# One core, two decoder layers: the weights' split into high and low parts, in two pieces a chunk instead of four

## The chip, the core and the metric

The kernel runs on one core of a Trainium2 chip. The metric is device time in microseconds (us) of one execution of the program; the figure given for a kernel is the median of its runs. The engines are called as the profile calls them: PE (TensorE, matmuls), PEld (its weight loads), DVE (VectorE), ACT (ScalarE), POOL (GpSimd) and SP (SyncE, which here only issues DMAs).

## The reference

A decoder trunk of two layers on x of shape (1, 256, 2048) in float32. Cut to what matters:

```python
for layer in range(2):
    if layer % 2 == 0:      # RG-LRU heads and RWKV-7 heads side by side
        h = rms_norm(x, even_norm)
        xa, ga, pb = split(h @ w_in)             # w_in: 2048 x 5408
        ya = rg_lru(causal_dwconv(xa), ...) * gelu(ga)
        yb = rwkv7_time_mix(pb, ...)             # 16 heads of 64
        x = x + concatenate([ya, yb]) @ w_out    # 2048 x 2048
    else:                   # mLSTM, chunkwise
        h = rms_norm(x, odd_norm)
        xm, z = split(h @ w_in)                  # 2048 x 8192
        q, k, v = block_diag(...)                # blocks of 4
        hs = head_layer_norm(mlstm_chunkwise(q, k, v, ...)) + skip * silu(causal_dwconv(xm))
        x = x + (hs * silu(z)) @ w_out           # 4096 x 2048
    h = rms_norm(x, ffn_norm)                    # gated FFN with a causal convolution
    u = silu(causal_dwconv(h @ w_gate)) * (h @ w_up)   # 2048 x 5632, twice
    x = x + u @ w_down                           # 5632 x 2048
out = rms_norm(x, final_norm)
```

Nearly all of the arithmetic is in the big projections, and each weight is used once.

## The kernel before

Activations lie transposed, features on the 128 partitions and the 256 positions along the free axis. Weights come from HBM in *chunks* of 128 x 2048 float32 (1 MB), 416 of them: 40 for the even layer's input projection (`ein`), 8 + 8 for its output projection (`eoa`, `eob`), 2 x 88 for gate and up (`fgu`), 2 x 44 for down (`fd`), 64 and 32 for the odd layer's input and output (`oin`, `oout`). A chunk holds 16 tiles of 128 columns; a tile is the stationary operand of the matmuls of one pair of a row block k and a column block m.

The matmuls take operands in a reduced float32 format (F32R). To keep the precision, a weight w is split into a high part `wh` (w cast to F32R, on ACT) and a low part `wl` (w - wh, on DVE), and an activation likewise. Three products are added: high x high, high x low and low x high. `mm3` does this for a tile; the activation's two parts stand side by side, so that one matmul of 512 columns with `wh` (L254, L257) gives two products and one of 256 columns with `wl` (L255) the third. In the narrow form, used when only 256 positions of PSUM are there for a sum, `wh` is used twice with 256 columns (L259, L260) and `wl` once (L261). `mm3_pair` (L311, L313) does two tiles at a time for the FFN.

`chunk` loads one chunk by a DMA on SP's queue into a `raw` buffer (two of them), and `parts_of` gives the `wh` and `wl` buffers (a pool of two each) and a function that splits the piece i of the chunk. `chunk` splits all pieces one after the other. A buffer of `wh` or `wl` comes free when PE has read its last tile. `load_x`, at the start, calls `parts_of` itself, with four pieces of 288 columns.

Callers of `chunk` are `project` (16 tiles, k = 0 to 15, into one output), `flat` (the output projections; for `eoa` and `eob` an output takes 8 tiles, so a chunk holds two outputs) and `flat_pairs` (FFN). After every four tiles, or every two pairs, they call `tick`, which advances the other work by a step: generators for the RWKV pairs, the RG-LRU, the convolutions and the mLSTM heads. So the program is written in an order in which the small work is interleaved with the tiles; the lists `WAITS`, `OWAITS` and so on at the head of the file say how many ticks each step lets pass.

The framework's scheduler then decides by a cost estimate of its own in which order each engine gets its instructions, and sets the semaphores. So the order on DVE, ACT and PE may differ from the order in the code, and depends on the instructions' sizes.

Small operations of the even layer that the prediction names: L593 to L617 prepare an RWKV pair (two heads) from its projections, and L596 is a PE matmul of that preparation, whose result L598 reads; L629 and L630 copy `uv` out of PSUM, for PE's L637 and L649; L651 to L658 build the blocks for the triangular inverse; L765 to L772 normalise a pair's output `y` (the variance `var`, its root `rsq` on POOL, L381); L409 is a tap of a convolution (`lru_x`), which PE's L822 (the RG-LRU gates) needs; L824 to L843 are the RG-LRU's own rows; L432 adds an output tile to the residual `res`; L201 and L202 split an activation into its two parts.

Of the kernel before, what the change touches and what calls it, by code (L numbers as in the profile page):

```python
# [42 lines left out]
WAITS = [2, 6, 1, 0, 2, 6, 12, 1, 1, 0, 1, 1, 1, 7]  # L43
ZSTEP = 7
EWIDE = False
PIECES = 4
SW = [4, 2]
OWAITS = [5, 2, 4]
AWAITS = [0, 4, 0, 1, 1, 3]
# [57 lines left out]
class Builder:  # L107
# [118 lines left out]

    def chunk(self, src, n=2048, pieces=PIECES):
        hi, lo, piece = self.parts_of(self.raw_load(src, n), pieces)
        for i in range(pieces):
            piece(i)  # L230
        return hi, lo
# [992 lines left out]
```

## Time and profile before

| | us |
|---|---|
| runs, not profiled | 2627.35, 2628.34, 2629.81 (median 2628.34) |
| the profiled execution's own time | 2631.14 |
| its span, first to last instruction | 2629.4 |

The stages follow one another in time, since each needs the whole of the one before:

| stage | us of the span |
|---|---|
| even layer, input projection with RWKV and RG-LRU | 0 to 380 |
| even layer, output projection | 380 to 517 |
| first FFN, up and down | 517 to 985, 985 to 1222 |
| odd layer, input projection with mLSTM, output projection | 1222 to 1700, 1700 to 1885 |
| second FFN, up and down | 1885 to 2372, 2372 to 2614 |
| final norm and output | 2614 to 2629.4 |

How to read the rows quoted below. A row of the timeline is: start and duration in us, engine, line of the kernel, operation, what it writes and reads, shapes, count, and in brackets how long the engine had been idle before it and which operation released it. A group's row ends with the number of instructions, their busy time in us, the mean of one in ns, and the idle time before them by what ended it. A row of waits is: total us, times, longest. In the rows by window the first two numbers are the stretch and its length, then each engine's busy time with its instructions, then the granted TensorE clock (1.00 is full speed), the DMA engines' busy share and GB/s.

### The profile page before, as it was taken

How to read it: one execution, taken by the hardware profiler on the slowest of the kernel's cores; microseconds unless marked ns; L12 is line 12 of the kernel's file. 1: busy time of each engine (PE TensorE's matmuls, PEld its weight loads, DVE VectorE, ACT ScalarE, POOL GpSimd, SP SyncE). 2: the span in 40 equal slices, each digit the busy share in tenths (PEclk: the TensorE clock that was granted, in tenths of full speed). 3: DMA queues.
4: the chain of work that ended last, by engine and by line, in shares of the span. 5: the costliest groups of instructions: out<-in, count | busy, mean ns of one | idle time of the engine just before them, and what ended most of it. 6: DMA issues, size and time to landing. Idle time of an engine off the chain costs nothing.

```text
span 2629.4 us, 42787 instructions
## 1 busy us (share of the span) xinstructions
PE 2600.2 (99%) x16214; PEld 2274.5 (87%) x16214; DVE 1865.2 (71%) x4261; ACT 1466.4 (56%) x3094; POOL 140.5 (5%) x417
## 2 busy tenths in 40 slices
PE   9999999999999999999999999999999999999997
PEld 8988887888888888888888888888888888888886
DVE  7988888888677765555777688865666667775554
ACT  6766663555555554444666667644455555554443
POOL 1222220000000000000000000000000000000000
PEclk9999999999999999999999999999999999999998
DMA  5433333455555555555444444455555555555553
GB/s 207 154 123 125 118 102 137 173 214 212 187 185 190 188 184 202 190 189 189 161 145 145 143 147 161 145 192 187 182 192 192 192 183 188 191 187 198 181 201 131
DMA packets 67694, 454.37 MB, mean 173 GB/s; under 512 B 9328, under 2 KB 10352, under 8 KB 14240
## 3 DMA queue, kind: packets, MB, share of 16 engines
q1 hardware_dynamic: 62064, 441.69, 47.6%
q0 software_dynamic: 4416, 7.85, 1.2%
q8 instruction: 127, 2.08, 0.3%
q10 hardware_dynamic: 1008, 2.11, 0.2%
q14 instruction: 79, 0.65, 0.1%
HBM read 448.70 MB, written 2.10 MB: 171 GB/s over the span
## 4 chain that ended last, share of the span: by engine, by line
PE 71%; issue 10%; DVE 0%; ACT 0%; POOL 0%; DVEq 0%; POOLq 0%; ACTq 0%
PE mp L311 31%; PE mp L313 15%; PE mm L257 14%; PE mm L255 8%; PE sc L934 1%; PE mm L254 1%; PE pv L919 1%; PE pz L1074 1%; PE pr L928 1%; PE pz L1075 0%; DVE res L1119 0%; PE pz L1052 0%; PE pt L397 0%; PE pt L1088 0%; PE pt L1065 0%
## 5 line engine op out<-in xcount | busy, mean ns | idle before, releaser
L244 DVE TENSOR_TENSOR wl<-raw,wh 128x512 fp32r<-128x512 f32 (+1 forms) x1680 | 1094.3, 684 | 506.2 <-ACT wh L243 505.3
L243 ACT CAST wh<-raw 128x512 fp32r<-128x512 f32 (+1 forms) x1680 | 956.0, 618 | 711.4 <-PE mp L311 510.9
L311 PE MATMUL mp<-x,wh 128*128 128x512 f32 x2816 | 884.7, 395 | 0.0
L313 PEld LDWEIGHTS mp<-x,wl 128*128 128x128 f32 x2816 | 529.0, 188 | 125.0
L313 PE MATMUL mp<-x,wl 128*128 128x256 f32 x2816 | 553.2, 278 | 0.0
L311 PE MATMUL mp<-ux,wh 128*128 128x512 f32 x1408 | 437.0, 392 | 0.0
L311 PEld LDWEIGHTS mp<-x,wh 128*128 128x128 f32 x2816 | 428.8, 189 | 0.1
L257 PE MATMUL mm<-x,wh 128*128 128x512 f32 x960 | 341.7, 394 | 0.0
L313 PEld LDWEIGHTS mp<-ux,wl 128*128 128x128 f32 x1408 | 264.4, 188 | 58.2
L255 PE MATMUL mm<-x,wl 128*128 128x256 f32 x1024 | 283.4, 287 | 0.0
L313 PE MATMUL mp<-ux,wl 128*128 128x256 f32 x1408 | 277.9, 279 | 0.0
L257 PE MATMUL mm<-yx,wh 128*128 128x512 f32 x720 | 259.5, 399 | 0.0
L255 PE MATMUL mm<-yx,wl 128*128 128x256 f32 x768 | 212.3, 287 | 1.9 <-DVE wl L244 1.0
L311 PEld LDWEIGHTS mp<-ux,wh 128*128 128x128 f32 x1408 | 213.2, 188 | 0.0
L257 PEld LDWEIGHTS mm<-x,wh 128*128 128x128 f32 x960 | 180.3, 188 | 35.9 <-DVE x L344 0.2
L255 PEld LDWEIGHTS mm<-x,wl 128*128 128x128 f32 x1024 | 193.2, 189 | 7.6 <-DVE yx L202 2.3
L259 PE MATMUL mm<-x,wh 128*128 128x256 f32 x640 | 193.2, 302 | 0.0
L261 PE MATMUL mm<-x,wl 128*128 128x256 f32 x640 | 182.5, 285 | 1.5 <-DVE wl L244 1.5
L260 PE MATMUL mm<-x,wh 128*128 128x256 f32 x640 | 181.4, 283 | 0.0
L257 PEld LDWEIGHTS mm<-yx,wh 128*128 128x128 f32 x720 | 137.1, 191 | 29.4
L255 PEld LDWEIGHTS mm<-yx,wl 128*128 128x128 f32 x768 | 145.9, 191 | 7.9 <-DVE wl L244 1.4
L259 PEld LDWEIGHTS mm<-x,wh 128*128 128x128 f32 x640 | 121.7, 190 | 6.7 <-ACT wh L243 0.2
(352 smaller groups left out, 2640.2 us busy)
## 6 DMA issues: line engine op xcount, KB each, us to landing
raw<-fgu SPq DMA_DIRECT2D x176, 1024.0 KB, 4.9
raw<-fd SPq DMA_DIRECT2D x88, 1024.0 KB, 4.8
raw<-oin SPq DMA_DIRECT2D x64, 1024.0 KB, 4.8
raw<-ein SPq DMA_DIRECT2D x40, 1024.0 KB, 5.0
raw<-oout SPq DMA_DIRECT2D x32, 1024.0 KB, 4.8
raw<-eoa SPq DMA_DIRECT2D x8, 1024.0 KB, 4.8
raw<-eob SPq DMA_DIRECT2D x8, 1024.0 KB, 4.8
wif<-wif POOLq DMA_DIRECT2D x12, 256.0 KB, 4.3
```

The costliest lines, as they stand in the source:

```text
L243: nc.scalar.copy(hi[:, s], raw[:, s])
L244: nc.vector.tensor_tensor(out=lo[:, s], in0=raw[:, s], in1=hi[:, s].bitcast(F32), op=ALU.subtract)
L254: TE.matmul(ps, hi, x, start=True, stop=False)
L255: TE.matmul(ps[:, 1], lo, x[:, 1], start=False, stop=False)
L257: TE.matmul(ps, hi, x, start=False, stop=stop)
L259: TE.matmul(ps, hi, x[:, 0], start=start, stop=False)
L260: TE.matmul(ps, hi, x[:, 1], start=False, stop=False)
L261: TE.matmul(ps, lo, x[:, 1], start=False, stop=stop)
L311: TE.matmul(ps[:, i], hi[i], x, start=start, stop=False)
L313: TE.matmul(ps[:, i, 1], lo[i], x[:, 1], start=False, stop=stop)
L919: TE.matmul(ps[:, s], xm[:, 3 + s * P:3 + s * P + P], bv, start=True, stop=True)
L928: TE.matmul(ps, bl, xc, start=True, stop=True)
```

## The change

`PIECES` is the default of `chunk`'s argument `pieces`: a chunk of 2048 columns is split in two pieces of 1024 columns, where it was four of 512. `load_x` is not touched.

```diff
 EWIDE = False
-PIECES = 4
+PIECES = 2
 SW = [4, 2]
 ...
     def chunk(self, src, n=2048, pieces=PIECES):
         hi, lo, piece = self.parts_of(self.raw_load(src, n), pieces)
         for i in range(pieces):
             piece(i)
         return hi, lo
```

On ACT and on DVE there are 832 instructions fewer each. The DMAs and PE's 15229 rows are the same in number, but the scheduler orders what lies between differently: some 570 of PE's rows stand at another place, by at most 32 places, nearly all of them in the even layer, and 995 of DVE's other rows, by at most 17. Three places on DVE follow, first as before, then as changed. The last two numbers of a name are buffer numbers and differ between the two.

At the first RWKV pair, some 60 us into the span, DVE before. `wl_112` is the chunk on which PE works; its first piece stands further up in both.

```order
L610 TENSOR_TENSOR ar_104_855<-r_81_722,ep_96_810 128x4x64
L604 SCALAR_TENSOR_TENSOR t0_103_852<-a_94_803,k_79_716 128x256
L605 SCALAR_TENSOR_TENSOR k_79_716<-t0_103_852,vec_sb_70,k_79_716 128x256
L598 TENSOR_SCALAR t1_102_847<-pw_101_845 128x256
L613 TENSOR_TENSOR bk_105_856<-k_79_716,epi_97_813 128x4x64
L617 SCALAR_TENSOR_TENSOR t1_106_863<-r_81_722,vec_sb_70,k_79_716 128x256
L244 TENSOR_TENSOR wl_112_886<-raw_110_883,wh_111_885 128x512 x3
L409 SCALAR_TENSOR_TENSOR lru_x_114_908<-xa_84_764,vec_sb_70,lru_x_114_908 128x256
L601 TENSOR_TENSOR kk_99_817<-kk_99_817,t1_102_847 128x256
```

The same place, DVE as changed:

```order
L610 TENSOR_TENSOR ar_104_835<-r_81_706,ep_96_790 128x4x64
L604 SCALAR_TENSOR_TENSOR t0_103_832<-a_94_783,k_79_700 128x256
L244 TENSOR_TENSOR wl_112_866<-raw_110_863,wh_111_865 128x1024
L598 TENSOR_SCALAR t1_102_827<-pw_101_825 128x256
L605 SCALAR_TENSOR_TENSOR k_79_700<-t0_103_832,vec_sb_70,k_79_700 128x256
L409 SCALAR_TENSOR_TENSOR lru_x_114_884<-xa_84_748,vec_sb_70,lru_x_114_884 128x256
L613 TENSOR_TENSOR bk_105_836<-k_79_700,epi_97_793 128x4x64
L617 SCALAR_TENSOR_TENSOR t1_106_843<-r_81_706,vec_sb_70,k_79_700 128x256
L409 SCALAR_TENSOR_TENSOR lru_x_114_884<-xa_84_748,vec_sb_70,lru_x_114_884 128x256
L244 TENSOR_TENSOR wl_127_960<-raw_125_957,wh_126_959 128x1024
```

The second piece of the chunk has moved up from behind L617 to right behind L604, and it now holds the tiles k = 8 to 15, where before the second held k = 4 to 7. On PE, L596 stood behind the tile k = 3 and now stands behind k = 8; the L822 that follow stand five tiles later than before.

At the end of the RWKV pair at 240 us, DVE before (`wl_545` is the current chunk, `y_475` the pair's output):

```order
L244 TENSOR_TENSOR wl_545_3395<-raw_543_3392,wh_544_3394 128x512
L765 TENSOR_TENSOR y_475_3007<-y_475_3007,st_536_3362 128x256
L427 TENSOR_TENSOR ga_540_3386<-mm_531_3310,bc_69_653 128x256
L244 TENSOR_TENSOR wl_545_3395<-raw_543_3392,wh_544_3394 128x512
L769 TENSOR_REDUCE var_538_3368<-lnsq_537_3366 128x4
L409 SCALAR_TENSOR_TENSOR lru_x_551_3429<-xa_527_3295,vec_sb_70,lru_x_551_3429 128x256
L770 TENSOR_SCALAR var_538_3368<-var_538_3368 128x4
L696 TENSOR_TENSOR zf_572_3537<-zc_493_3145,con_even_sb_358 128x512
L772 TENSOR_TENSOR y_475_3007<-y_475_3007,rsq_539_3371 128x256
L629 COPY uv_549_3421<-pw_550_3422 64x2x64
L409 SCALAR_TENSOR_TENSOR lru_x_551_3429<-xa_527_3295,vec_sb_70,lru_x_551_3429 128x256
L629 COPY uv_549_3421<-pw_550_3422 64x2x64
```

The same place, DVE as changed:

```order
L244 TENSOR_TENSOR wl_545_3295<-raw_543_3292,wh_544_3294 128x1024
L612 TENSOR_TENSOR bk_523_3173<-kk_512_3115,epi_510_3111 128x4x64
L765 TENSOR_TENSOR y_475_2919<-y_475_2919,st_536_3262 128x256
L427 TENSOR_TENSOR ga_540_3286<-mm_531_3210,bc_69_637 128x256
L409 SCALAR_TENSOR_TENSOR lru_x_551_3325<-xa_527_3199,vec_sb_70,lru_x_551_3325 128x256
L769 TENSOR_REDUCE var_538_3268<-lnsq_537_3266 128x4
L409 SCALAR_TENSOR_TENSOR lru_x_551_3325<-xa_527_3199,vec_sb_70,lru_x_551_3325 128x256
L770 TENSOR_SCALAR var_538_3268<-var_538_3268 128x4
L629 COPY uv_549_3317<-pw_550_3318 64x2x64
L772 TENSOR_TENSOR y_475_2919<-y_475_2919,rsq_539_3271 128x256
L409 SCALAR_TENSOR_TENSOR lru_x_551_3325<-xa_527_3199,vec_sb_70,lru_x_551_3325 128x256
L629 COPY uv_549_3317<-pw_550_3318 64x2x64
```

The two narrow pieces around L765 have become one wide piece ahead of it, L612 has come in, the 512-column L696 has gone elsewhere, and one of the two copies of `uv` stands ahead of L772.

At the start of the output projection, 387 us, DVE before (`wl_933` is the first chunk of `eoa`; its first piece stands further up in both):

```order
L653 TENSOR_TENSOR gk_908_5425<-pw_911_5436,con_even_sb_358 64x256
L655 TENSOR_TENSOR gr1_912_5444<-pw_911_5436,con_even_sb_358 128x256
L658 TENSOR_REDUCE dc_913_5446<-zd_906_5423 128x64
L843 SCALAR_TENSOR_TENSOR ga_897_5393<-t0_922_5472,ga_897_5393 128x256
L244 TENSOR_TENSOR wl_933_5506<-raw_931_5503,wh_932_5505 128x512
L834 SCALAR_TENSOR_TENSOR lru_i_918_5459<-lru_i_918_5459,lru_x_902_5407 128x256
L244 TENSOR_TENSOR wl_933_5506<-raw_931_5503,wh_932_5505 128x512
L832 SCALAR_TENSOR_TENSOR lru_t_920_5462<-t1_921_5463,lru_t_920_5462 128x256
L244 TENSOR_TENSOR wl_933_5506<-raw_931_5503,wh_932_5505 128x512
```

The same place, DVE as changed:

```order
L653 TENSOR_TENSOR gk_908_5265<-pw_911_5276,con_even_sb_358 64x256
L655 TENSOR_TENSOR gr1_912_5284<-pw_911_5276,con_even_sb_358 128x256
L658 TENSOR_REDUCE dc_913_5286<-zd_906_5263 128x64
L843 SCALAR_TENSOR_TENSOR ga_897_5233<-t0_922_5312,ga_897_5233 128x256
L244 TENSOR_TENSOR wl_933_5346<-raw_931_5343,wh_932_5345 128x1024
L832 SCALAR_TENSOR_TENSOR lru_t_920_5302<-t1_921_5303,lru_t_920_5302 128x256
L834 SCALAR_TENSOR_TENSOR lru_i_918_5299<-lru_i_918_5299,lru_x_902_5247 128x256
```

What stands behind L843 was the second piece, with the second half of the first output's tiles; it is now the second output's piece, and the whole first output is in the piece further up.

## The prediction

> **What bounds the kernel now.** I read the page's first line, then the busy time by stage, then the list of what TensorE waited for, then the split's own instructions, and last a few timelines where a chunk of weights begins. The page's first part gives each engine's busy time:
>
> ```profile
> PE 2600.2 (99%) x16214; PEld 2274.5 (87%) x16214; DVE 1865.2 (71%) x4261; ACT 1466.4 (56%) x3094; POOL 140.5 (5%) x417
> ```
>
> PE is busy 2600.2 of 2629.4 us, so 29 us is all that any cover could give back. Where those 29 us lie is shown by the windows, cut at the stage borders: the even layer's input projection (0 to 380), its output projection (380 to 517), the first FFN's up and down halves, and the odd layer's input projection (1222 to 1700).
>
> ```profile
> core 0: us, PE busy (x) PEld busy (x) DVE busy (x) ACT busy (x) POOL busy (x), PEclk, DMA share, GB/s
> 0.00:380.00 380.00, 371.38 (x3250) 334.51 (x3250) 325.28 (x943) 256.16 (x551) 78.85 (x181) 1.00 0.42 142
> 380.00:517.00 137.00, 131.69 (x869) 105.51 (x868) 114.13 (x297) 66.29 (x147) 13.17 (x23) 0.96 0.40 137
> 517.00:985.00 468.00, 468.00 (x2690) 408.41 (x2689) 347.18 (x734) 262.38 (x550) 11.00 (x54) 1.00 0.55 196
> 985.00:1222.00 237.00, 237.00 (x1374) 208.44 (x1374) 133.51 (x244) 108.41 (x210) 0.68 (x2) 1.00 0.55 195
> 1222.00:1700.00 478.00, 477.89 (x2789) 418.39 (x2788) 361.48 (x897) 311.77 (x701) 25.53 (x105) 1.00 0.43 151
> ```
>
> The FFN and the odd layer show no gap in PE. The even layer has 380.00 - 371.38 = 8.6 and 137.00 - 131.69 = 5.3 us, and there DVE is busy 86% and 83%. So only the even layer can react to DVE's timing, unless the change makes a gap where none is. What ended the gaps, from the list of waits on PE (its eight longest rows):
>
> ```profile
> PE pw L637 <- ACT uv L630: 3.8, 4, 1.0
> PE mm L370 <- DVE ssq L359: 2.7, 1, 2.7
> PE pc L776 <- DVE y L772: 1.6, 2, 0.8
> PE mm L261 <- DVE wl L244: 1.5, 1, 1.5
> PE mm L135 <- DVE warm L132: 1.5, 1, 1.5
> PE mm L397 <- DVE dg L396: 1.4, 1, 1.4
> PE mm L255 <- DVE wl L244: 1.0, 1, 1.0
> PE pw L822 <- DVE lru_x L409: 0.9, 1, 0.9
> ```
>
> PE waits for a split piece (wl, written at L244) twice in the whole run, 1.5 and 1.0 us. The rows on the FFN's matmuls, L311 and L313, are missing: these never wait for a piece. The rest are waits on chains of small operations.
>
> **The change: 832 casts and 832 subtractions fewer, each left over twice as wide.** The price of a wide one comes from the groups kept apart by shape, the 256-column rows of the same two operations giving the slope:
>
> ```profile
> L244 DVE TENSOR_TENSOR wl<-raw,wh 128x512 fp32r<-128x512 f32 x1664 | 1087.5, 686 | 506.0 <-ACT wh L243 505.1
> L243 ACT CAST wh<-raw 128x512 fp32r<-128x512 f32 x1664 | 949.8, 620 | 711.1 <-PE mp L311 510.9 <-PE mm L257 94.2 <-PE mm L260 55.4
> L202 DVE TENSOR_TENSOR ux<-u,ux 128x256 fp32r<-128x256 f32 x88 | 36.9, 419 | 0.0
> L201 ACT CAST ux<-u 128x256 fp32r<-128x256 f32 x88 | 35.5, 403 | 0.0
> ```
>
> On DVE (686 - 419) / 256 = 1.04 ns a column, so 1024 columns take 686 + 534 = 1220 ns; on ACT (620 - 403) / 256 = 0.85 ns, so 620 + 434 = 1054 ns. A chunk costs DVE 2 x 1220 = 2440 instead of 4 x 686 = 2744 ns, ACT 2108 instead of 2480. Over 1664 / 4 = 416 chunks DVE loses 126 us of busy time, ACT 155. PE covers all of it: it is the busy engine, and its matmuls stay the same. That term is 0.
>
> **The first piece comes later.** The cast is 434 ns and the subtraction 534 ns longer, so the first lo piece is ready 0.97 us later after the chunk's buffer came free. The timeline of the FFN's down half shows what room there is (start, duration, engine, line):
>
> ```profile
> 1204.88 2.19 ACT L243 CAST wh<-raw 128x512 fp32r<-128x512 f32 x4 [3.33 <-PE mp L311]
> 1205.53 2.50 DVE L244 TENSOR_TENSOR wl<-raw,wh 128x512 fp32r<-128x512 f32 x4 [3.02 <-ACT wh L243]
> 1210.39 0.62 ACT L243 CAST wh<-raw 128x512 fp32r<-128x512 f32 x1 [3.33 <-PE mp L311]
> 1210.42 0.62 PE L311 MATMUL mp<-ux,wh 128*128 128x512 f32 x2
> ```
>
> The cast starts when PE lets go of the buffer (3.33 us idle before it, ended by L311), and again 5.5 us later, which is one chunk's period. The first lo piece is done at 1205.53 + 0.69 = 1206.2; PE takes the chunk at 1210.42. That leaves 4.2 us, and 0.97 more is no wait. The FFN's up half and the odd layer have the same two buffers and so the same period, with DVE busy 74% and 76% beside it; no row of the wait list comes from them. Term 0. The raw buffer comes free a little earlier or later by the same tenths of a microsecond, ahead of a DMA that is 0.42 to 0.55 busy: 0.
>
> **Start of the first RWKV pair.** The timeline there:
>
> ```profile
> 60.45 1.65 ACT L243 CAST wh<-raw 128x512 fp32r<-128x512 f32 x3
> 62.41 1.89 DVE L244 TENSOR_TENSOR wl<-raw,wh 128x512 fp32r<-128x512 f32 x3
> 63.15 0.38 PE L261 MATMUL mm<-x,wl 128*128 128x256 f32 x1 [1.54 <-DVE wl L244]
> ```
>
> DVE does the pair's preparation before the second piece, which PE needs at the chunk's fifth tile; that is the 1.54 us wait. In the changed order the first piece serves eight tiles, and the second stands right behind L604, with L605, L613 and L617 behind it. PE reaches the ninth tile four tiles later and the piece is earlier. I take -1.4: the 1.54, less what a piece longer by 0.53 still delays. The two L822 matmuls, which wait 0.94 now, stand five tiles later and can win that too; L598, on which the pair's chain hangs, gets 0.53 later and can lose as much. Range -2.4 to 0, nearest the row of the wait itself.
>
> **Start of the output projection.** Its timeline:
>
> ```profile
> 387.73 0.70 PE L822 MATMUL pw<-lru_x,lru_w 128*128 128x256 f32 x2 [0.56 <-ACT lru_r L824]
> 388.70 0.68 DVE L244 TENSOR_TENSOR wl<-raw,wh 128x512 fp32r<-128x512 f32 x1
> 389.43 0.40 PE L255 MATMUL mm<-yx,wl 128*128 128x256 f32 x1 [1.01 <-DVE wl L244]
> ```
>
> Here again PE waits 1.01 us for the second piece of a chunk whose eight first tiles make one output. With 1024 columns a piece holds all eight, and it already stands ahead of the L651 to L658 rows. Term -1.0; 0 if the longer first piece pushes those rows, and so L822's next inputs, by as much.
>
> **Four sites at the ends of later pairs.** The wait of L637 for uv, 3.8 us in four times. One of them (a chain from var over POOL to y and uv):
>
> ```profile
> 239.59 1.41 POOL L381 TENSOR_TENSOR rsq<-var,minus_half 128x4 f32<-128x4 f32 x1 [3.93 <-DVE var L770]
> 241.03 0.43 DVE L772 TENSOR_TENSOR y<-y,rsq 128x256 f32<-128x256 f32 x1 [0.94 <-POOL rsq L381]
> 242.71 0.55 PE L637 MATMUL pw<-con_sb,bk 128*128 128x128 f32 x3 [0.98 <-ACT uv L630]
> ```
>
> POOL runs alone for 1.41 us, and DVE idles 0.94 of that. In the changed order a whole 1024-column piece stands ahead of L765, and a row L612 between them: 0.53 + 0.43 (L772's duration for as many columns) later at worst, +1.0. But one of the two uv copies (L629) moves ahead of L772 into the POOL wait, at best 0.43 earlier by the same row. The middle is +0.3, times four +1.2; range -1.7 to +3.8.
>
> **Inside the output projection.** A chunk in the steady state:
>
> ```profile
> 484.12 1.65 ACT L243 CAST wh<-raw 128x512 fp32r<-128x512 f32 x3
> 485.68 1.28 DVE L244 TENSOR_TENSOR wl<-raw,wh 128x512 fp32r<-128x512 f32 x2
> 487.10 0.40 PE L255 MATMUL mm<-yx,wl 128*128 128x256 f32 x2
> ```
>
> The first lo piece is ready at 485.68 + 0.68 = 486.36, and PE first uses it at 487.10: 0.74 us to spare, the least room of any steady stretch, because DVE puts residual rows ahead of the piece. A subtraction 0.53 us longer just fits; a later cast as well (0.97) would miss it by 0.23 a chunk. In the changed order the piece stands one to three residual rows earlier, so I take two of the 16 chunks missing by 0.23, +0.5. Range 0 to +3.7, all 16.
>
> The Trainium skill ("Perfetto Trace Analysis", section "Optimizing Scalar/DVE Operations") says that where Scalar and Vector aren't saturated but cause bubbles on other engines, breaking instructions up may let work be completed sooner. That speaks against this change, at the bubbles above. By it the sum would be that of the first rival below, 2636.8; the trace has two such bubbles, both at a second piece, which the change takes off PE's way, so I don't follow it.
>
> **PE's waits that are already satisfied.** The built order has half as many L311 and L313 rows that carry a wait. Whether such a wait costs PE anything is read from pairs of the FFN's up half:
>
> ```profile
> 620.25 0.63 PE L311 MATMUL mp<-x,wh 128*128 128x512 f32 x2
> 620.94 0.63 PE L311 MATMUL mp<-x,wh 128*128 128x512 f32 x2
> 621.64 0.62 PE L311 MATMUL mp<-x,wh 128*128 128x512 f32 x2
> ```
>
> Pairs of tiles start 0.69 and 0.70 us apart, and every second one begins a new piece. So it costs 0, or at most the 0.01 between them: two pairs a chunk in 264 FFN chunks, 5.3 us either way.
>
> **The clock.** PE runs at half clock in two stretches:
>
> ```profile
> 389.60:393.00 3.40, 3.40 (x12) 2.92 (x13) 3.40 (x8) 2.44 (x5) 1.56 (x3) 0.51 0.20 34
> 468.10:475.00 6.90, 6.32 (x19) 4.96 (x20) 5.70 (x14) 4.33 (x11) 0.24 (x1) 0.51 0.24 67
> ```
>
> They cost 0.49 x 10.3 = 5 us, and the first starts right behind the 1.01 us wait. If that wait goes, half of 3.4 us may go too; another stretch may as well appear behind a new wait. I take 0, range -5 to +3.4. The Trainium skill ("TensorE: Matmul & The Clock Gate", section "HAM oscillation") ties the half clock to idle gaps of more than about 3.4 us. By that rule a wait of 1 us could not bring it on, and the clock's term would be 0 with no range; the trace differs, since its first stretch stands behind 1.01 us.
>
> **Sum:** -1.4 - 1.0 + 1.2 + 0.5 = -0.7 us. The profiled execution took 2631.14 us (its span is 2629.4), so 2630.4; that execution lies 2.8 above the median of the three runs, 2628.34. Against the median the forecast is 2627.6 us.
>
> **Rivals.**
>
> *Slower: the late first piece in the output projection.* Each of its 16 chunks starts its cast when PE frees a buffer, so a miss repeats in every chunk. For it: the 0.74 us of room is less than 0.97. Against it: the piece moves ahead of residual rows, each of which is worth up to 0.43 us (L772's duration, as many columns). It decides once the room is under 0.97; with the room used up, each chunk pays the subtraction's 0.53: 16 x 0.53 = 8.5, time 2636.8. Chance 0.16.
>
> *Faster: a lighter DVE shortens the chains.* The even layer has 56 chunks, on which DVE saves 56 x 0.30 = 17 us in stretches where it is 83 to 86% busy. Half of PE's 8.6 + 5.3 us of gaps, 7.0, would go: 2621.3. For it: most waits in the list are for DVE's small rows. Against it: the scheduler fills DVE's program with wide pieces that can't be cut, and the saving falls into 0.97 us of later first pieces. Chance 0.15.
>
> *No change to the program in effect.* Excluded: the built order has the wide rows.
>
> **How the numbers follow.** About 0.2%, 5.3 us, is what a measurement of this kernel can tell from no change. My forecast, gaps that shift by a microsecond or two, has a chance of 0.69, and its own range is 2623 to 2633.5. The faster rival lies below that, the slower above: 0.15, 0.69 and 0.16. The range for 8 times in 10 leaves out about 0.1 on each side: low 2620, the faster rival's time with a part of the clock's; high 2637, the slower rival's.
>
> **What would show it.** In the profile after: L244 x832 with about 1220 ns and L243 about 1054 ns; DVE busy near 1740 and ACT near 1310 us; PE busy still near 2600; the wait of L261 and L255 for wl gone from the list; L637's four waits between 0.5 and 2.0 us each; no wait of L311 or L313 on wl. Wrong, if L255 or L257 waits at every chunk between 393 and 517 us (first rival), if the pairs of the FFN come closer than 0.69 us, or if the stretches at half clock change in number.

## The result, and the profile after

With two pieces a chunk the kernel takes 2650.45 us (median; 2647.69 to 2651.25), against 2627.85 for the kernel before, run beside it on the same chip: a ratio of 1.0086 with a 95% interval of 1.0074 to 1.0098, or 19 to 26 us slower. The forecast was 2627.6, in a range of 2620 to 2637. The page's first line after:

```profile
PE 2608.9 (98%) x16214; PEld 2281.4 (86%) x16214; DVE 1831.2 (69%) x3429; ACT 1400.6 (53%) x2262; POOL 141.8 (5%) x417
```

DVE and ACT did get lighter, by 34 and 66 us, and PE's idle time grew all the same, from 29.2 to 40.0 us (2629.4 - 2600.2 and 2648.9 - 2608.9). The two groups of the split (instructions, busy us, mean ns, idle time before them):

```profile
L244 DVE TENSOR_TENSOR wl<-raw,wh 128x1024 fp32r<-128x1024 f32 x832 | 1004.4, 1220 | 534.3 <-ACT wh L243 532.4
L243 ACT CAST wh<-raw 128x1024 fp32r<-128x1024 f32 x832 | 856.3, 1048 | 726.5 <-PE mp L311 518.5 <-PE mm L257 116.1 <-PE mm L260 76.9
```

1220 and 1048 ns are the slope's prices to within 6 ns, so the parts' costs were right. Where the time went is shown by the windows at the borders used before (even layer's input projection, its output projection, first FFN up), though the three stages now end some 14 to 18 us later:

```profile
0.00:380.00 380.00, 363.79 (x3129) 327.13 (x3130) 312.13 (x827) 236.22 (x444) 76.70 (x175) 0.98 0.41 139
380.00:517.00 137.00, 130.64 (x893) 105.41 (x894) 108.25 (x270) 66.96 (x123) 15.00 (x28) 0.96 0.35 121
517.00:985.00 468.00, 466.85 (x2683) 407.17 (x2682) 342.49 (x572) 250.84 (x379) 11.33 (x53) 1.00 0.56 196
```

PE's gaps in the input projection are 380.00 - 363.79 = 16.2 us, where they were 8.6, and its mean clock fell from 1.00 to 0.98. The other two stretches add 1.1 and 1.2 us of gaps. The longest waits of PE, and two shorter ones that are new as well:

```profile
PE pw L666 <- DVE tq L707: 6.6, 4, 2.8
PE pw L637 <- ACT uv L630: 4.3, 4, 1.1
PE mm L370 <- DVE ssq L359: 2.7, 1, 2.7
PE pc L776 <- DVE y L772: 2.3, 2, 1.4
PE mm L261 <- DVE wl L244: 1.7, 4, 1.0
PE pw L666 <- DVE zf L696: 1.7, 2, 1.3
...
PE mp L313 <- DVE wl L244: 1.1, 1, 1.1
...
PE pw L674 <- DVE gk L653: 0.7, 1, 0.7
```

The first row is new, and no row of the prediction spoke of it. L666 makes three products one after the other for a pair, to build the rest of a triangular inverse: of `zf`, of a first `tq` and of a second `tq`. DVE's L707 turns their results into the first `tq`, the second `tq` and `tt`. The second `tq` is late in four pairs. The stretches at half clock have grown as well (the third number from the end is the granted clock):

```profile
81.20:88.00 6.80, 6.56 (x34) 5.92 (x31) 6.80 (x10) 4.26 (x11) 5.43 (x7) 0.54 0.48 163
265.20:268.80 3.60, 3.53 (x30) 3.24 (x30) 1.92 (x10) 0.24 (x1) 0.00 (x0) 0.57 0.73 291
350.80:357.70 6.90, 6.90 (x29) 6.01 (x28) 4.16 (x10) 2.35 (x5) 0.54 (x1) 0.55 0.01 2
398.00:405.00 7.00, 7.00 (x31) 6.21 (x31) 6.64 (x14) 2.27 (x5) 2.71 (x5) 0.51 0.05 16
486.40:490.20 3.80, 3.29 (x11) 2.31 (x10) 3.17 (x7) 2.75 (x5) 0.00 (x0) 0.55 0.34 113
```

Each stretch times the missing share of the clock: 3.1 + 1.5 + 3.1 + 3.4 + 1.7 = 12.9 us. Three of these windows begin 0.3 to 0.6 us late. In the trace's clock records the five stretches last 6.83, 3.41, 6.83, 6.83 and 3.41 us at a clock of 0.50, so the full loss is 13.7 us, against 5.1 before. Gaps (7.6 + 1.1 + 1.2 = 9.9) and clock (8.5) make 18.4 of the 19.5 us between the two spans, 2648.9 and 2629.4.

Why `tq` is late is shown by DVE's timeline at the worst of the four, in the changed kernel:

```profile
262.51 0.57 DVE L681 TENSOR_TENSOR zz<-blocks,con_even_sb 32x256 f32<-32x256 f32 x1 [3.00 <-DMA blocks<-dc]
263.01 0.40 DVE L844 SCALAR_TENSOR_TENSOR y<-ga,y 128x256 f32<-128x256 f32 x1
263.34 1.20 DVE L244 TENSOR_TENSOR wl<-raw,wh 128x1024 fp32r<-128x1024 f32 x1
264.47 0.41 DVE L778 TENSOR_TENSOR y<-y,bonus 128x256 f32<-128x256 f32 x1
264.81 0.40 DVE L707 TENSOR_TENSOR tq<-pw,zf 128x256 f32<-128x256 f32 x1
```

L681 begins the inverse of the *next* pair and needs `blocks`, which POOL sends by DMA. DVE works in order, so it stood idle for 3.00 us with the wide piece and `tq` in the queue behind, though PE had finished the product for `tq` at 260.65. POOL's row and PE's wait beside it:

```profile
254.65 2.44 POOL L660 DMA_DIRECT2D blocks<-dc  x4
```

```profile
265.27 1.01 PE L666 MATMUL pw<-tq,ze 64*64 64x64 f32 x14 [2.75 <-DVE tq L707]
```

The last of the four DMAs was issued by 257.1, and L681 could start at 262.5. The transfers themselves did not get slower: these DMAs take 2.6 us from issue to landing in the median and 5.9 at most, where they took 2.7 and 5.6. At the same place before, from DVE's timeline, `tq` was done at 256.3 and L681 stood behind `tt`, where the blocks had landed and it waited for nothing:

```profile
255.92 0.42 DVE L707 TENSOR_TENSOR tq<-pw,zf 128x256 f32<-128x256 f32 x1
...
257.91 0.42 DVE L707 TENSOR_TENSOR tt<-pw,zf 128x256 f32<-128x256 f32 x1 [0.31 <-PE pw L666]
258.25 0.58 DVE L681 TENSOR_TENSOR zz<-blocks,con_even_sb 32x256 f32<-32x256 f32 x1
```

So the first theory: the scheduler, with other sizes to plan with, put L681 of four pairs ahead of the second `tq`; DVE then waits for a DMA, and PE for DVE. The rival: the wide pieces themselves come late, wherever they are.

### The profile page after: what moved, and what is told of

The parts are those of the page before. It is cut to its first block, busy times and chain, and to the rows that moved or that the text cites. A ratio compares the mean times of both kernels' runs of the same rounds, so it can differ in the third digit from the quotient of the medians.

```text
span 2648.9 us, 41233 instructions
## 1 busy us (share of the span) xinstructions
PE 2608.9 (98%) x16214; PEld 2281.4 (86%) x16214; DVE 1831.2 (69%) x3429; ACT 1400.6 (53%) x2262; POOL 141.8 (5%) x417
## 4 chain that ended last, share of the span: by engine, by line
PE 70%; issue 10%; DVE 1%; DMA 0%; ACT 0%; POOL 0%; DVEq 0%; POOLq 0%; ACTq 0%
PE mp L311 30%; PE mp L313 15%; PE mm L257 13%; PE mm L255 7%; PE sc L934 1%; PE mm L254 1%; PE pv L919 1%; PE pz L1074 1%; PE pr L928 1%; DMA wif<-wif 0%; DVE wl L244 0%; PE pz L1075 0%; DVE res L1119 0%; PE pz L1052 0%; PE pt L397 0%
## 5 line engine op out<-in xcount | busy, mean ns | idle before, releaser
L244 DVE TENSOR_TENSOR wl<-raw,wh 128x1024 fp32r<-128x1024 f32 (+1 forms) x848 | 1011.1, 1205 | 534.8 <-ACT wh L243 532.9
L243 ACT CAST wh<-raw 128x1024 fp32r<-128x1024 f32 (+1 forms) x848 | 862.5, 1037 | 727.2 <-PE mp L311 518.5
L313 PEld LDWEIGHTS mp<-x,wl 128*128 128x128 f32 x2816 | 528.9, 188 | 126.5 <-DVE wl L244 1.6
L313 PE MATMUL mp<-x,wl 128*128 128x256 f32 x2816 | 553.3, 278 | 1.1 <-DVE wl L244 1.1
L313 PEld LDWEIGHTS mp<-ux,wl 128*128 128x128 f32 x1408 | 264.4, 188 | 58.2
L255 PE MATMUL mm<-x,wl 128*128 128x256 f32 x1024 | 283.6, 287 | 0.0
L313 PE MATMUL mp<-ux,wl 128*128 128x256 f32 x1408 | 277.9, 279 | 0.0
L255 PE MATMUL mm<-yx,wl 128*128 128x256 f32 x768 | 211.7, 286 | 2.0 <-ACT yx L201 1.6
L255 PEld LDWEIGHTS mm<-x,wl 128*128 128x128 f32 x1024 | 193.2, 189 | 7.5 <-issue 2.9
L259 PE MATMUL mm<-x,wh 128*128 128x256 f32 x640 | 195.2, 305 | 0.0
L261 PE MATMUL mm<-x,wl 128*128 128x256 f32 x640 | 185.1, 289 | 1.7 <-DVE wl L244 1.7
L255 PEld LDWEIGHTS mm<-yx,wl 128*128 128x128 f32 x768 | 145.0, 190 | 7.8 <-ACT yx L201 2.1
L259 PEld LDWEIGHTS mm<-x,wh 128*128 128x128 f32 x640 | 123.7, 193 | 7.6 <-issue 0.2
```

The lines of the kernel that those rows point to most:

```text
L243: nc.scalar.copy(hi[:, s], raw[:, s])
L244: nc.vector.tensor_tensor(out=lo[:, s], in0=raw[:, s], in1=hi[:, s].bitcast(F32), op=ALU.subtract)
L255: TE.matmul(ps[:, 1], lo, x[:, 1], start=False, stop=False)
L259: TE.matmul(ps, hi, x[:, 0], start=start, stop=False)
L261: TE.matmul(ps, lo, x[:, 1], start=False, stop=stop)
L313: TE.matmul(ps[:, i, 1], lo[i], x[:, 1], start=False, stop=stop)
```

## The experiments

**Which layers.** Two kernels that have two pieces in one part of the program only. In both, `chunk` takes its number from a flag, which is set where the output projection has ended:

```diff
-    def chunk(self, src, n=2048, pieces=PIECES):
+    def chunk(self, src, n=2048):
+        pieces = 2 if self.two else 4
...
             self.flat(self.io["eob"], 8, KD, yx[8:], ...)
+            self.two = True      # False in the second kernel
```

> Two pieces in the FFN and the odd layer, four in the even layer. Order theory (in the even layer the scheduler moved L681, which waits for a DMA, ahead of the second tq row on DVE): the even layer is as before, so the time is 2628 to 2631, with no wait of L666 for tq. Width theory (wide pieces come later and PE waits for them wherever they are): 376 - 16 of the 416 chunks are wide, so most of the loss stays, 2640 or more, spread over the span.

> The reverse: two pieces in the even layer, four in the FFN and the odd layer. Order theory: nearly the whole loss, 2646 to 2651, with the wait of L666 for tq near 6.6 us in four times. Width theory: 56 of 416 chunks are wide, a loss of a few us, 2629 to 2634.

Measured: late2 2629.32 us, ratio 1.0007 (0.9998 to 1.0016); even2 2647.99, ratio 1.0079 (1.0065 to 1.0092). The 360 wide chunks of the FFN and the odd layer cost nothing that can be measured, the 56 of the even layer nearly all. So a wide piece has no cost that comes with every chunk. Whether wide pieces cost by themselves inside the even layer is not settled by these two.

**L681 alone, both ways.** First the changed kernel with L681 tied behind the `tt` of the pair before, for four pairs (an order on DVE's queue, without a wait); then the kernel before with L681 written early and the second `tq` tied behind it:

```diff
# p2_tz, PIECES = 2
-        V.tensor_tensor(out=Z, in0=DT..., op=ALU.add)
+        with self.tc.issue_after(self.last_t) if 3 <= j <= 6 else ExitStack():
+            V.tensor_tensor(out=Z, in0=DT..., op=ALU.add)
...
+            if n == 2:
+                self.last_t = q.ins       # q: the L707 row that writes tt
# p4_ze1, PIECES = 4
-        yield from wait(WAITS[5])
-        V.tensor_tensor(out=Z, in0=DT..., op=ALU.add)
+        yield from wait(1)
+        self.last_z = V.tensor_tensor(out=Z, in0=DT..., op=ALU.add)
+        yield from wait(WAITS[5] - 1)
...
+            order = self.tc.issue_after(self.last_z.ins) if n == 1 and 2 <= j <= 5 else ExitStack()
+            with order:
                 V.tensor_tensor(out=tt, in0=ps, in1=zt, op=ALU.add)
```

> Two pieces everywhere, with L681 of four pairs tied behind the row tt of the pair before on DVE, where it stood with four pieces. Order theory: the four waits of L666 for tq (6.6 us) go, and with them part of the half clock that follows such waits: 2634 to 2642. Width theory: DVE's wide pieces stay, so the waits change their names and the time stays at 2646 to 2651.

> Four pieces everywhere, with L681 of five pairs put ahead of the second tq on DVE, as the changed kernel has it. Order theory: L681 idles DVE for the DMA with narrow pieces too; from the profile of before, blocks land some 1.6 us after tq is done now, so L666 waits 1 to 2 us in four or five pairs: 5 to 10 us, with half clock behind some of them up to 15, 2634 to 2643. Width theory: no wide piece, so 2626 to 2631.

Measured: p2_tz 2639.29, ratio 1.0044 (1.0032 to 1.0057); p4_ze1 2634.83, ratio 1.0024 (1.0014 to 1.0034). With wide pieces and L681 tied, PE's list has no row of L666 for tq any more; its first rows are

```profile
PE pw L637 <- ACT uv L630: 3.9, 4, 1.1
PE mm L370 <- DVE ssq L359: 2.7, 1, 2.7
PE pc L779 <- DVE y L775: 2.3, 2, 1.4
```

and half of the loss, 11 of 22.6 us, is gone. In the profiles PE's idle time falls from 40.0 to 32.6 us and its busy time by 4.3, with three stretches at half clock where there were five. With narrow pieces and L681 early, the waits are there, from DVE's list and PE's:

```profile
DVE zz L681 <- DMA blocks<-dc: 5.5, 5, 1.8
```

```profile
PE pw L666 <- DVE tq L710: 3.7, 4, 1.4
```

So the order makes PE wait at either width: DVE's 5.5 us became 3.7 us on PE. The time rose by 7 us, which these waits do not cover: PE idles 32.2 us in this profile, against 29.2 in the first profile of the kernel before and 30.4 in its second. In the changed kernel DVE's row was

```profile
DVE zz L681 <- DMA blocks<-dc: 7.2, 4, 3.0
```

and a wide piece stands there between L681 and `tq`. That more of the wait reaches PE (6.6 of 7.2 us, against 3.7 of 5.5) goes with that, but was not tried by itself.

**The same order, without tying a row.** The kernel before with one number changed, `WAITS[5]` from 6 to 7.

> Four pieces everywhere; the only edit is that L681 and what follows it in its pair are written one tick (four tiles) later, WAITS[5] 7 instead of 6. In this build the scheduler puts L681 between the two tq rows in five pairs, as in the changed kernel. Order theory: waits of L666 for tq of 1 to 3 us in four or five pairs, 2634 to 2645. Width theory: 2626 to 2631, no such waits.

Measured: 2634.96, ratio 1.0029 (1.0017 to 1.0040). The time is in the range, but not by the expected way:

```profile
DVE zz L681 <- DMA blocks<-dc: 1.9, 1, 1.9
```

```profile
PE pw L666 <- DVE tq L707: 1.7, 1, 1.7
```

L681 stands ahead of `tq` in five pairs and waits in one, since it comes a tick later itself and the blocks have mostly landed by then. One wait of DVE, one of PE: the row's place on the queue makes PE wait for `tq` only where the DMA is late. The rest of its 7 us is not accounted for here. Since it loses as much as p4_ze1 with a single such wait, the 7 us of p4_ze1 are not shown to be the price of its four.

**Width on DVE alone.** The cast in four pieces, the subtraction in two:

```diff
             nc.scalar.copy(hi[:, s], raw[:, s])
-            nc.vector.tensor_tensor(out=lo[:, s], in0=raw[:, s], ...)
+            if n != 2048:       # load_x: as before
+                nc.vector.tensor_tensor(out=lo[:, s], in0=raw[:, s], ...)
+            elif i % 2:
+                s = slice(i * w - w, i * w + w)
+                nc.vector.tensor_tensor(out=lo[:, s], in0=raw[:, s], ...)
```

> The subtraction on DVE in two pieces, the cast on ACT in four. In this build the scheduler leaves L681 behind the second tq in all pairs of the input projection. Order theory: no wait of L666 for tq above 1 us, and 2627 to 2635, the upper end if the second pair's start is at half clock. Width theory: DVE's pieces are as wide as in the changed kernel, 2642 to 2650.

Measured: 2653.08, ratio 1.0093 (1.0078 to 1.0109). That missed the order theory's range by far, and lies above the width theory's too. The order theory's particular held: no L666 of the four middle pairs waits for tq, and between chunk 12 and chunk 35 of the input projection the delay against the kernel before, read at the same tile in both traces, goes only from 12.7 to 13.4 us. But new waits stand at the start and at the output projection, from PE's list and DVE's:

```profile
PE pw L600 <- ACT t L597: 3.8, 2, 2.3
PE mm L265 <- DVE wl L248: 3.4, 3, 2.4
PE mm L259 <- DVE wl L248: 3.4, 2, 2.7
```

```profile
DVE zz L685 <- DMA blocks<-dc: 6.7, 2, 4.4
```

(L685, L600, L265 and L259 are the L681, L596, L261 and L255 of the other kernels.) Two of these rows, L265's and L259's, and 2.4 us of L313 as well, are waits for a split piece itself, so in this kernel late wide pieces are not excluded as a cause beside the order. That L681 is ahead of `tq` is one place to lose time, not the only one.

**The rest of the loss.** The changed kernel with the first ten chunks in four pieces, without and with L681 tied; then the 16 chunks of the output projection in four pieces as well; and these 16 alone in two:

```diff
+        self.two += 1
+        pieces = 4 if 1 <= self.two <= 10 else 2
# and with the output projection
+        pieces = 4 if self.two <= 10 or 41 <= self.two <= 56 else 2
```

> Four pieces in the first ten chunks, two in the others, L681 not tied. If the start and the four pairs are separate losses, the start's 4.5 us go and the rest stays: 2644 to 2648, with the waits of L666 for tq at 6 to 8 us in four times. If the pairs' order followed from the start's, both go: 2633 to 2638.

> L681 of four pairs tied behind tt, and four pieces in the first ten chunks, two in the others. Half-clock theory (what is left of the loss with L681 tied is mostly the half clock at 80 to 87 us, which follows waits at the start of the second RWKV pair): no stretch at half clock between 60 and 100 us, and the time falls from 2639 to 2633 to 2637. If the rest of the loss is spread over the wide chunks instead: 2638 to 2641.

> L681 of four pairs tied behind tt, four pieces in the first ten chunks and in the 16 of the output projection, two in the other 390. If the three places (the four pairs, the start, the output projection) hold the loss, 2629 to 2632. If wide pieces cost something everywhere as well, 2633 or more.

> Two pieces in the 16 chunks of the even layer's output projection alone. The slower rival of the prediction (each late first piece there costs PE up to 0.53 us): 2634 to 2637. Order theory (the loss stands at the pairs of the input projection): 2627 to 2631.

| kernel | us | ratio (95% interval) |
|---|---|---|
| changed | 2650.45 | 1.0086 (1.0074 to 1.0098) |
| p2_h10: first ten chunks in four | 2644.84 | 1.0066 (1.0053 to 1.0078) |
| p2_tz: L681 tied | 2639.29 | 1.0044 (1.0032 to 1.0057) |
| p2_tz_h10: both | 2634.78 | 1.0023 (1.0014 to 1.0033) |
| p2_tz_h10_eo4: and the output projection in four | 2630.15 | 1.0010 (1.0001 to 1.0019) |
| eo2: only the output projection in two | 2630.93 | 1.0009 (1.0000 to 1.0017) |

In p2_h10 L666 still waits 7.8 us for tq in four times (its line numbers are higher by three):

```profile
PE pw L669 <- DVE tq L710: 7.8, 4, 2.5
```

So the start's loss and the pairs' are separate. The pieces of the loss add up: about 11 us for L681, 5 for the first ten chunks (whether L681 is tied or not), 3 for the output projection, and 3 for the other 390 chunks, an amount that reaches down to nothing. In p2_tz_h10 the input projection is level with the kernel before, though 30 of its 40 chunks are wide:

```profile
0.00:380.00 380.00, 371.57 (x3251) 334.22 (x3251) 325.20 (x885) 250.95 (x491) 77.46 (x181) 1.00 0.42 142
```

PE 371.57 here and 371.38 before: wide pieces in these places cost PE nothing. Most of the loss of the first ten chunks is clock in the profiles. With them narrow, PE's idle time is 38.9 us instead of 40.0 and its busy time 4.8 us less; with L681 tied as well, 32.0 instead of 32.6 and 2.1 less. A half-clock stretch of 6.83 us that begins at 80 to 83 us stands in the four profiles in which these chunks are wide on ACT and DVE (after, after_again, even2, p2_tz). It follows L674's wait of 0.7 us for `gk` (78 us; in the list above), which also stands in these four alone. That this wait brings the half clock on was not tried, and whether it comes by the order or by the late piece was not taken apart.

**The clock.** The two kernels once more, for a second profile each.

> The changed kernel once more, for a second profile. 2648 to 2652. If the half clock follows fixed places, its stretches stand again at 80, 265, 350, 398 and 487 us; if it comes by chance behind waits, the one at 80 (seen in three kernels) stands and others move.

> The kernel before once more, for a second profile: 2626 to 2631; half clock again at 389 and at 468 us, or moved, by the same two cases.

Measured: 2649.72, ratio 1.0084 (1.0070 to 1.0098), and one run of the kernel before, 2628.74. The two largest rows of waits came again to a tenth of a microsecond in sum, though not pair by pair (1.7, 2.8, 1.7 and 0.5 us for `tq` in the first profile, 0.6, 2.6, 1.7 and 1.7 in the second):

```profile
PE pw L666 <- DVE tq L707: 6.5, 4, 2.6
PE pw L637 <- ACT uv L630: 4.3, 4, 1.1
```

The half clock did not come again at all the same places; in the second profile of the changed kernel it stands here:

```profile
82.50:89.50 7.00, 6.28 (x30) 6.28 (x31) 7.00 (x14) 3.34 (x10) 5.08 (x7) 0.51 0.63 202
202.00:210.00 8.00, 8.00 (x57) 7.06 (x57) 5.36 (x13) 2.97 (x6) 1.34 (x3) 0.57 0.11 17
318.00:321.50 3.50, 3.50 (x20) 3.16 (x19) 2.46 (x10) 2.06 (x3) 0.00 (x0) 0.51 0.65 267
399.80:403.50 3.70, 3.70 (x18) 3.26 (x15) 3.60 (x9) 1.57 (x4) 0.90 (x2) 0.54 0.00 0
485.50:492.50 7.00, 6.49 (x20) 5.16 (x21) 4.89 (x11) 3.42 (x6) 0.14 (x1) 0.53 0.22 67
```

Three of five places are the same, two have moved to other pairs, and the sum is the same, 13.6 us (13.7 in the clock records, as in the first profile). The kernel before had one stretch in its second profile, near 470 us, and two in its first.

## Why the prediction was wrong

It forecast no change, and the kernel became 23 us slower. Point by point:

- *The pieces' prices* (1220 and 1054 ns forecast, 1220 and 1048 measured): right. The saving worked out from them was too large: DVE's busy time fell by 34 us and not 126, ACT's by 66 and not 155 (1831 and 1401 us, where 1740 and 1310 were forecast). Count times mean duration overstates it, since successive rows of one engine overlap: in the prediction's own row four pieces take 2.50 us, and not 4 x 0.686 = 2.74. The faster rival's 17 us came from the same sum. The 0 for the load itself was right, as PE covers it.
- *The 0 for the FFN and the odd layer, and for PE's satisfied waits*: right to within late2's interval, up to 0.16%; in it 360 chunks have half the waits. Not to the letter: L313 waits once for `wl`, 1.1 us in the first FFN (at 556 us), where the prediction expected no such wait. That wait is not in late2, and is 0.4 us in eo2, so it goes with wide pieces in the output projection before it. L255 waits 0.4 us for `wl` once in the odd layer (at 1728 us), and late2 has that one too.
- *The first RWKV pair*, forecast -1.4: right in its place, where 0.24 of the 1.54 us wait is left. But L261 now waits for `wl` four times, 1.7 us in all for 1.5, and the same ten chunks cost 5 us more, behind rows that the prediction did not look at.
- *The start of the output projection*, -1.0: the 1.01 us wait of L255 for `wl` is gone there. But L776 waits 1.4 us for `y` instead of 0.8, L666 1.3 for `zf` instead of 0.3, and, at 484 us, L255 1.6 for `yx` instead of 0.9. No gain in sum.
- *The four sites of L637*, +1.2: 4.3 us instead of 3.8, so +0.5 and well sized.
- *Inside the output projection*, +0.5 in 0 to +3.7: eo2 shows 0 to 4.5 us, middle 2.4. The slower rival's 8.5 us, in which every late piece counts, is excluded by that time, and by eo2's list, in which PE waits for `wl` once in the whole output projection (1.4 us, at its start).
- *The clock*, 0 in -5 to +3.4: +8.5 us. This term was mis-sized, because it was bounded by the two stretches seen before and the number of waits was taken to stay.
- *The step that failed* is the one in which the reordering was priced. The prediction went through three sites where DVE's order had changed, and all three were places where PE already waited. L681's move is a change at a place where nothing waited before; in the built order it stood there to be read, at four pairs, and the row's input comes by DMA. No term and no rival spoke of it, so a place without a wait was priced at nothing without a reason. It is worth 11 of the 22.6 us, with the clock that goes with it. Of the other half, 5 us lie in the first ten chunks and 3 in the output projection, and there the cause is only narrowed down; 3 more, in the other 390 chunks, are hardly clear of the noise.

The Trainium skill's rule in "Perfetto Trace Analysis" ("Optimizing Scalar/DVE Operations") pointed the right way, slower, and I had given it the first rival's price. The runs agree with its direction but not with the reason taken for it: where the order was held, wide pieces cost PE nothing (371.57 us busy of 380), and the largest bubbles, L666's, came from a row that was put ahead. In dve2, where PE waits for `wl` at the start and at the output projection, that is not settled.

## What to carry to other kernels

Where a scheduler sets the order, a change of instruction size is also a change of order; go through every row that moved and ask first which of them waits for a DMA, since an engine that works in order makes everything behind that row wait too. A place with no wait before can hold one after, so the list of waits bounds what can be won and not what can be lost. If the size is wanted and the order is not, tie the moved row where it stood and measure again.

## What the runs showed of the hardware

The half clock was not expected to depend on waits this short. Apart from a longer one in the final norm and output, its stretches are 3.41 or 6.83 us long in all profiles, and they come behind some of PE's waits of 0.7 to 2.8 us and not behind others. At four places one profile of the changed kernel has a stretch and the other has none, though the wait ahead of it is the same to 0.2 us (1.06 and 1.06, 2.75 and 2.58, 1.65 and 1.68, 1.07 and 1.06). Within one profile the stretches begin whole multiples of 3.413 us apart (80.56, 264.88, 350.21, 398.00 and 486.75 us: 54, 25, 14 and 26 of them), and in the second profile the same beat lies elsewhere. So where a wait falls on that beat may decide; this was not tried. In sum the stretches follow the number of waits, roughly: 5.1 and 1.7 us lost in the two profiles before, 13.7 in each of the two after, and none of it in the input projection of p2_tz_h10, where PE's busy time is that of before. The Trainium skill ("TensorE: Matmul & The Clock Gate", section "HAM oscillation") gives idle gaps of more than about 3.4 us as the cause; here the longest gap of PE in these stages is 2.8 us, so the measurement differs.
